# One load line for matrices and weights, and smaller weight steps, in the first stage of a fused diffusion block

## Chip, cores and metric

The kernel runs on one core of one Trainium2 chip. The metric is the device time of one launch in microseconds (us), as the median of runs. TensorE, VectorE, ScalarE, GpSimd and SyncE are called PE, DVE, ACT, POOL and SP in the profile; a DMA is issued by one of them into its queue.

## What is computed

One layer of a transformer block over 512 latent tokens of width 2048 (and 256 context tokens), in float32. Cut to what the first stage needs:

```
shift, scale, gate = split(silu(c) @ w_ada + b_ada, 3)       # modulation, per channel
h  = rmsnorm(x, norm_g) * (1 + scale) + shift                # 512 x 2048
p  = h @ w_in                                                # q, k, v, z_a, u_b, z_b, gates
y_b = (fourier_mix(u_b) * silu(z_b)) @ w_pb                  # branch B
...                                                          # attention branch A, merge, w_o, residual, final norm
```

The first stage makes `h` (transposed: 16 row blocks of 128 channels, each by 512 tokens) and from it u_b and z_b, eight strips of 128 columns of `w_in`. The Fourier part follows, then the large products.

## The kernel before

Each float32 operand of a product is split into a high and a low part (`split_from`: ACT writes the high part, L162, DVE the low part, L163), and one product is three matmuls (`mm3`, L296 to L298).

**A row block.** For block `kb`, `modulation(kb)` loads a matrix of 2 MB as two halves (`wada_load`, L416; tile `wa`, four buffers, so that two blocks fit) and multiplies it by the two condition vectors (L484, 16 matmuls for each half, 32 in all). ACT copies the sum (L491), PE turns it with two transposes (L494), and DVE reduces it and makes shift and gain (L500, L537, L538). `make_h` then scales the row on DVE (L472), writes the high part on ACT (L473) and the low part on DVE (L474). From then on the block can be multiplied.

**The weights.** The eight strips come in pieces of up to 512 KB (`start_pieces`, tile `wr`, four raw buffers), with the rows grouped as in

```
GROUPS = [(0, 1), (1, 1), (2, 2), (4, 4), (8, 4), (12, 4)]      # (first row block, how many)
```

A piece holds one group's rows for as many strips as fit. Strips 0 to 3 (u_b) keep a sum each in PSUM over all rows (`pb`). Strips 4 to 7 (z_b) are summed in PSUM over one group only (`pc`, two banks) and then added to `part`: by ACT's copy for the first row (L511), by DVE's addition later (L513). `start_work` is a generator that yields after each strip; the loop over `kb` draws from it up to what is owed, which counts whole groups only, and at most 32 matmuls a round.

**The loads.** Pieces are issued on SP. They are taken from the list `todo` by `load_more`, as far as raw buffers are free. The matrices of blocks 0 and 1 are issued on SP too, those of blocks 2 to 15 on POOL. `split_piece` splits pieces when `get` asks for them, `look` pieces ahead; in rounds 2 and 3 one further piece is split behind the row's own instructions (`tc.issue_after`).

**The order.** A scheduler places each engine's instructions from the order in which the program names them, their dependences and costs of its own; each engine then runs its list in order. `tc.issue_after(i)` keeps the next instructions behind `i`.

Of the kernel before, what the change touches and what calls it, by code (L numbers as in the profile page):

```python
# [18 lines left out]
P = 128  # L19
# [3 lines left out]
KK = D // P  # L23
# [13 lines left out]
START = [O_UB + P * i for i in range(4)] + [O_ZB + P * i for i in range(4)]  # L37
NS = len(START)

GROUPS = [(0, 1), (1, 1), (2, 2), (4, 4), (8, 4), (12, 4)]  # L40
RAW = 4

HL, MORE_HL = 3, 2
# [21 lines left out]
def context_piece(g, name, pc):  # L65

    n = 28 * (g - NQZ) + 4 * ONE_GROUP.index(name) + pc
    if n % 2 == 0 and 0 <= n < 8:
        return "cn", n // 2
    if n % 6 == 0 and 18 <= n < 42:  # L70
        return "cr", n // 6 - 3
# [18 lines left out]
def start_pieces():  # L90


    off, r = 0, []
    for kb, nk in GROUPS:
        per = 8 // nk
        new = [(kb, nk, t, min(per, NS - t)) for t in range(0, NS, per)]
        if kb == 0:

            new = [(0, 1, 0, 2), (0, 1, 2, 6)]
        for p in new:  # L100
            cols = p[1] * p[3] * P
            r.append((off, cols) + p)
            off += cols * P
    return r


# [1 line left out]
def block_kernel(ctx, tc, xT, ctx_rows, ctx_toks, x, c_row, w_ss, w_gate, vecs, qkg, rope, dft_c, dft_s,  # L108
                 w_start, w_g, w_pab, w_o, final_g, out):
    nc = tc.nc  # L110
# [8 lines left out]
    wp = sb("wp")  # L119
# [18 lines left out]
    def uid(s):  # L138
        cnt[0] += 1
        return f"{s}{cnt[0]}"  # L140
# [8 lines left out]
    def hm_tile(shape, dt, name):  # L149
        return slot(hm, shape[1:], dt)  # L150
# [4 lines left out]
    def bank2():  # L155
        return ps.tile([P, 512], F32, tag="b2", bufs=2, name=uid("pd"))
# [4 lines left out]
    def split_from(src, hi, lo):  # L161
        nc.scalar.activation(hi, src, ACT.Copy)  # L162
        return nc.vector.tensor_tensor(lo, src, hi.bitcast(F32), op=ALU.subtract)  # L163


    todo, ahead = [], []
# [16 lines left out]
    def start_load():  # L183

        e = todo[0]
        if callable(e):
            if e():
                todo.pop(0)
                return True
            return False  # L190
        used = [p for a in ahead for p, _ in a.raws]
        free = [p for p in raw_pools for _ in range(p[1] - used.count(p))]
        if len(e.parts) > len(free) or e.stage == 0 and (not chain or left[e.pc]):
            return False
        todo.pop(0)
        for p, src in zip(free, e.parts):
            raw = p[0].tile([P, 1024], F32, tag=p[2], bufs=p[3], name=uid("wr"))[:, : e.cols]
            nc.sync.dma_start(raw if len(src.shape) == 2 else raw.rearrange("p (i j c) -> p i j c", i=4, j=2), src)
            e.raws.append((p, raw))
        if e.stage == 0:  # L200
            nc.sync.dma_start(chain[e.pc], e.first)
            left[e.pc] = 1
        ahead.append(e)
        return True

    def load_more():
        while todo and len(ahead) < 8 and start_load():
            pass

    class Halves:  # L210

# [10 lines left out]
    def hl_tiles():  # L222
        hl_pools.append(hl_pools.pop(0))
        pool = hl_pools[-1]
        if isinstance(pool, tuple):
            return [slot_tile(p, (1024,), F32R) for p in pool]
        if isinstance(pool, int):
            return int_tiles(pool)
        return [pool.tile([P, 1024], F32R, tag=t, bufs=hl_pools.count(pool), name=uid("w" + t)) for t in ("hi", "lo")]
# [3 lines left out]
    look = [1]  # L233

    def split_piece(e):
        if e.out is not None or e.kind == "raw":
            return
        raws = [r for _, r in e.raws]
        src = raws.pop(0) if e.stage is None else chain[e.pc]
        for r in raws:  # L240
            nc.vector.tensor_tensor(src, src, r, op=ALU.add)
        if e.off:
            nc.vector.tensor_tensor(src, chain[e.pc], src, op=ALU.subtract)
        hi, lo = e.dst() if e.dst else hl_tiles()
        if isinstance(hi, Halves):
            for k in range(2):
                split_from(src[:, 512 * k : 512 * k + 512].rearrange("p (a c) -> p a c", a=2), hi.parts[k], lo.parts[k])
        else:
            hi, lo = hi[:, : e.cols], lo[:, : e.cols]
            last_split[0] = split_from(src, hi, lo)  # L250
        if e.nxt is not None:
            nc.gpsimd.dma_start(chain[e.pc], e.nxt, accum_op=ALU.add)  # L252
        if e.stage == 3:
            left[e.pc] = 0
        r = lambda t: t if isinstance(t, Halves) else t.rearrange("p (n m) -> p n m", n=e.n)
        e.out = (r(hi), r(lo))
# [111 lines left out]
    for g in range(LAST + 1):  # L368
        for name in ONE_GROUP:
# [6 lines left out]
            for pc in range(4):  # L376
                p = context_piece(g, name, pc)
                if p:
                    src, cols = (ctx_toks[p[1]], 1024) if p[0] == "cn" else (ctx_rows[p[1]], 4 * C)
# [14 lines left out]
    for name in OUT_GROUP:  # L394
        stream_product(name, 8, w_o[1], BY_DVE_OUT)
        if name in DONE:
            half, c = DONE[name]
            stream(("x", half, 2 + c), flat(x[half, 2 + c]), 1024, 1, "raw")
    for name in ONE_GROUP:
        stream_product(name, 9, w_o[0], BY_DVE_OUT)  # L400
        half, c = {"P2": (0, 0), "P7": (1, 1), "Q3": (1, 0)}.get(name, (0, 0))
# [11 lines left out]

    def wada_load(kb, h):
        w = pap.tile([P, 8, 256], F32, tag="wada", bufs=4, name=uid("wa"))
        (nc.gpsimd if kb > 1 else nc.sync).dma_start(w, w_ss[kb, :, 8 * h : 8 * h + 8, :])  # L416
        return w

    for a, n in XCH:
# [39 lines left out]
    def spread(pick, r):  # L459
# [2 lines left out]
            nc.tensor.matmul(acc[:, t * P : t * P + P], pick[:, t, :], r, start=True, stop=True)  # L462
        return acc

    wada = {(0, h): wada_load(0, h) for h in range(2)}
    while todo and len(ahead) < 3:
        start_load()
    wada.update({(1, h): wada_load(1, h) for h in range(2)})

    def make_h(hi, lo, src, rr, kb, j):  # L470
        tmp = src
# [6 lines left out]
    def matvec(acc, pieces):  # L478

        kk = 0  # L480
        for w in pieces:
            for k in range(w.shape[1]):
                j = kk % 4
                nc.tensor.matmul(acc[32 * j : 32 * j + 32, :256], c2[:, kk, :], w[:, k, :],  # L484
                                 start=kk < 4, stop=kk >= KK - 4)
                kk += 1

    def columns(acc, kb):

        o = pap.tile([P, 256], F32, tag="ada_o", bufs=2, name=uid("ado"))  # L490
        nc.scalar.copy(o, acc[:, :256])  # L491
        sp = acc[:, 256:]
        for i in range(2):
            turned = nc.tensor.transpose(sp[:, P * i : P * i + P], o[:, P * i : P * i + P], ident)  # L494
        if kb == 0:
            with tc.issue_after(turned.ins):
                rx0.append(spread(*norms))
            warm(3, o)
        r = pap.tile([P, 2, 2], F32, tag="ada_r", bufs=2, name=uid("adr"))
        nc.vector.tensor_reduce(r, sp.rearrange("p (h g r) -> p h r g", h=2, g=4)[:, :, 0:2, :], axis=AX.X, op=ALU.add)  # L500
        return r
# [30 lines left out]

    def modulation(kb):
        acc = bank2()
        matvec(acc, [wada.pop((kb, h), None) or wada_load(kb, h) for h in range(2)])
        sp = columns(acc, kb)
        nc.vector.tensor_scalar(shift[:, kb, :], sp[:, 0, :], bada[:, kb : kb + 1], None, op0=ALU.add)  # L537
        nc.vector.tensor_scalar(gain[:, kb, :], sp[:, 1, :], bsc1[:, kb : kb + 1], ng[:, kb : kb + 1],  # L538
                                op0=ALU.add, op1=ALU.mult)
# [18 lines left out]
    for kb in range(KK):  # L558
        if kb:
            modulation(kb)  # L560
        if kb % 2 == 0:
            pairs.append([hm_tile([P, 2, T], F32R, name=uid(n)) for n in ("hh", "hl")])
        hhi[kb], hlo[kb] = (t[:, kb % 2, :] for t in pairs[-1])
        ins = make_h(hhi[kb], hlo[kb], xt[:, kb, :], rx if kb else rx0[0], kb, 0)
        if kb >= 8:
            form_row(kb - 8)
        if kb == 0:
            nc.scalar.copy(rx, rx0[0])
            split_piece(ahead[0])
            with tc.issue_after(ins[1].ins):  # L570
                for e in ahead[1:3]:
                    split_piece(e)

        full = max([k + n for k, n in GROUPS if k + n <= kb] or [0])
        owed = 24 * full
        lim = min(owed, done + 32)
        while done < lim:
            done += next(work)
        if kb in (2, 3):
            with tc.issue_after(ins[1].ins), tc.issue_after(ins[2].ins):  # L580
                split_piece(next(e for e in ahead if e.out is None))
            look[0] = 2 * kb - 2
    while next(work):
        pass
    pa.close()
    rp = ctx.enter_context(tc.tile_pool(name="rp", bufs=1, reuse_waits="tile"))
    chain += [rp.tile([P, 1024], F32, name=f"R{pc}") for pc in range(4)]
# [18 lines left out]
    raw = get(("dftc", 0))  # L606
# [270 lines left out]
    class Context:  # L877
# [8 lines left out]
        def begin(self, name):  # L886
            self.f = get(("cf", name))
            if name == "Q5":
                nc.sync.dma_start(self.K.rearrange("p (h d) -> p h d", h=4), qkg[:, 2:3, :].broadcast_to([P, 4, HD]))
# [296 lines left out]
    for i in range(NSTEP + 3):  # L1186
        h, t = divmod(i, 4)
# [381 lines left out]
```

## Time and profile before

| | us |
|---|---|
| three runs | 1332.83, 1335.85, 1336.69 |
| median | 1335.85 |
| the profiled execution | 1333.12 |
| its span, first to last instruction | 1331.3 |

The span is what the views of the profile divide; the profiled execution's time holds 1.8 us more around it. In a timeline row stand start, duration, engine, line, operation, output and inputs, shape and count; in brackets the idle time of the engine just before, and what ended it. A matmul's duration runs past the start of the next, since they are pipelined; its cost is the distance between starts.

### The profile page before, as it was taken

To read this page: it belongs to the slowest core of one execution; us is meant where nothing else is said; L and a number is where in the kernel's file an instruction comes from. 1 tells how busy PE (TensorE), PEld (TensorE's weight loads), DVE (VectorE), ACT (ScalarE), POOL (GpSimd) and SP (SyncE) were. 2 spreads that over 40 slices of the span, in tenths; PEclk is the share of its full clock that TensorE was granted. 3 is DMA by queue.
4 is the path that set the end of the run, shared out by engine and by line. 5 is a ranking of instruction groups with operands and counts; after the bars stand their busy time and mean duration, and the time that the engine had idled before them with its cause. 6 is when DMAs were issued, how large, how long until landed. Compare 5 with 4: busy or idle time off the path is not lost. (4 is left out here: it accounts for less than half of the span.)

```text
span 1331.3 us, 17479 instructions
## 1 busy us (share of the span) xinstructions
PE 1298.5 (98%) x6594; PEld 1061.9 (80%) x6594; DVE 977.9 (73%) x1286; ACT 653.2 (49%) x1017; POOL 137.1 (10%) x186
## 2 busy tenths in 40 slices
PE   6999999999999999999999999999999999999996
PEld 3566888888888887888887888788888888887885
DVE  4655989887778867646477666677776789777677
ACT  5322655555555544544264455666665133364444
POOL 1110011210302011011021110000000100111210
PEclk9999999999999999999999999999999999999999
DMA  9996677887897999777669886122113899678983
GB/s 380 402 387 243 227 190 197 228 230 223 195 317 189 304 268 267 255 166 182 190 181 308 217 240 227 31 71 80 43 53 112 328 329 333 181 172 224 224 216 142
DMA packets 96085, 291.28 MB, mean 219 GB/s; under 512 B 8960, under 2 KB 32000, under 8 KB 91648
## 3 DMA queue, kind: packets, MB, share of 16 engines
q1 hardware_dynamic: 51600, 172.95, 37.1%
q0 software_dynamic: 21936, 94.39, 29.0%
q10 hardware_dynamic: 22464, 22.81, 5.1%
q8 instruction: 52, 0.85, 0.3%
q14 instruction: 33, 0.27, 0.1%
HBM read 263.37 MB, written 26.75 MB: 218 GB/s over the span
## 5 line engine op out<-in xcount | busy, mean ns | idle before, releaser
L162 ACT ACTIVATE whi<-wr 128x1024 fp32r<-128x1024 f32 (+1 forms) x130 | 136.6, 1052 | 189.8 <-PE y L298 90.0
L296 PE MATMUL y<-whi,s 128*128 128x512 f32 x548 | 216.4, 395 | 1.1 <-ACT s L768 1.1
L297 PE MATMUL y<-wlo,s 128*128 128x512 f32 x548 | 214.0, 390 | 0.7 <-DVE wlo L163 0.7
L296 PE MATMUL x<-whi,s 128*128 128x512 f32 x548 | 214.1, 391 | 0.2 <-ACT s L765 0.2
L297 PE MATMUL x<-wlo,s 128*128 128x512 f32 x548 | 213.5, 390 | 0.1
L298 PE MATMUL y<-whi,s 128*128 128x512 f32 x548 | 213.4, 390 | 0.0
L298 PE MATMUL x<-whi,s 128*128 128x512 f32 x548 | 213.3, 389 | 0.0
L163 DVE TENSOR_TENSOR wlo<-wr,whi 128x1024 fp32r<-128x1024 f32 (+1 forms) x130 | 157.0, 1211 | 57.6 <-ACT whi L162 57.4
L162 ACT ACTIVATE whi<-R 128x1024 fp32r<-128x1024 f32 x115 | 121.6, 1059 | 128.3 <-PE y L298 55.5
L163 DVE TENSOR_TENSOR wlo<-R,whi 128x1024 fp32r<-128x1024 f32 x115 | 139.7, 1220 | 48.9 <-ACT whi L162 48.9
L296 PEld LDWEIGHTS y<-whi,s 128*128 128x128 f32 x548 | 102.9, 188 | 24.9 <-DVE s L1166 2.3
L296 PEld LDWEIGHTS x<-whi,s 128*128 128x128 f32 x548 | 102.9, 188 | 21.8 <-ACT s L765 0.5
L297 PEld LDWEIGHTS x<-wlo,s 128*128 128x128 f32 x548 | 102.9, 188 | 21.7 <-DVE wlo L163 0.6
L298 PEld LDWEIGHTS y<-whi,s 128*128 128x128 f32 x548 | 102.9, 188 | 21.6
L298 PEld LDWEIGHTS x<-whi,s 128*128 128x128 f32 x548 | 102.9, 188 | 21.4
L297 PEld LDWEIGHTS y<-wlo,s 128*128 128x128 f32 x548 | 103.0, 188 | 20.4 <-DVE wlo L163 1.1
L296 PE MATMUL x<-s,s 128*128 128x512 f32 (+1 forms) x274 | 104.5, 381 | 4.2 <-ACT s L1126 3.1
L297 PE MATMUL x<-s,s 128*128 128x512 f32 (+1 forms) x284 | 106.5, 375 | 0.0
L298 PE MATMUL x<-s,s 128*128 128x512 f32 (+1 forms) x284 | 106.1, 374 | 0.0
L252 POOL DMA_DIRECT2D R<-in_w_g x64 | 55.2, 863 | 423.6 <-DVE wlo L163 263.2
L162 ACT ACTIVATE s<-wr 128x512 fp32r<-128x512 f32 (+2 forms) x92 | 60.4, 675 | 57.4 <-PE y L298 17.2
L163 DVE TENSOR_TENSOR s<-wr,s 128x512 fp32r<-128x512 f32 (+2 forms) x92 | 65.8, 743 | 23.3 <-ACT s L162 21.8
(275 smaller groups left out, 2249.0 us busy)
## 6 DMA issues: line engine op xcount, KB each, us to landing
wr<-in_w_g SPq DMA_DIRECT2D x128, 512.0 KB, 4.9
R<-in_w_g POOLq DMA_DIRECT2D x64, 512.0 KB, 6.7
wa<-in_w_ss POOLq DMA_DIRECT2D x28, 1024.0 KB, 9.1
R<-in_w_g SPq DMA_DIRECT2D x32, 512.0 KB, 5.1
wr<-in_w_pab SPq DMA_DIRECT2D x32, 512.0 KB, 5.1
wr<-in_w_gate SPq DMA_DIRECT2D x32, 512.0 KB, 5.5
wr<-in_w_o SPq DMA_DIRECT2D x24, 512.0 KB, 6.9
R<-in_w_o POOLq DMA_DIRECT2D x24, 512.0 KB, 7.4
```

The lines of the kernel that those rows point to most:

```text
L162: nc.scalar.activation(hi, src, ACT.Copy)
L163: return nc.vector.tensor_tensor(lo, src, hi.bitcast(F32), op=ALU.subtract)
L252: nc.gpsimd.dma_start(chain[e.pc], e.nxt, accum_op=ALU.add)
L296: nc.tensor.matmul(o, ah, bh, start=start, stop=False, skip_group_check=cont)
L297: nc.tensor.matmul(o, ah, bl, start=False, stop=False, skip_group_check=cont)
L298: nc.tensor.matmul(o, al, bh, start=False, stop=stop, skip_group_check=cont)
```

## The change

The steps are written out. Rows 0 to 3 come one by one, rows 4 to 11 in twos, and of the last four rows strips 0 to 3 in twos and strips 4 to 7 in one group. The round owes each step as soon as its rows are made. All loads of the stage, matrices too, are issued on SP, each kept behind the one before it: after each matrix follow as many pieces as `BEHIND` says. A matrix is asked for when the one two blocks earlier has been multiplied. From round 2 on, each round splits one piece behind its row's own instructions, and `look` stays at 1 until the stage ends.

```diff
-GROUPS = [(0, 1), (1, 1), (2, 2), (4, 4), (8, 4), (12, 4)]
+STEPS = ([(0, 1, 0, 2), (0, 1, 2, 6)] + [(k, 1, 0, 8) for k in range(1, 4)]
+         + [(k, 2, t, 4) for k in range(4, 12, 2) for t in (0, 4)] + [(12, 2, 0, 4), (14, 2, 0, 4)]
+         + [(12, 4, t, 2) for t in (4, 6)])
+BEHIND = {**{k: 1 for k in range(2, 14)}, 14: 2, 15: 2}
...
-            nc.sync.dma_start(raw if len(src.shape) == 2 else raw.rearrange("p (i j c) -> p i j c", i=4, j=2), src)
+            dst = raw if len(src.shape) == 2 else raw.rearrange("p (i j c) -> p i j c", i=4, j=2)
+            begin = lambda: nc.sync.dma_start(dst, src)
+            if may[0] < 1000:
+                in_line(begin)
+            else:
+                begin()
...
+    may, last_load = [0], [None]
+
+    def in_line(dma):
+        if last_load[0] is None:
+            last_load[0] = dma()
+        else:
+            with tc.issue_after(last_load[0].ins):
+                last_load[0] = dma()
+
     def load_more():
-        while todo and len(ahead) < 8 and start_load():
-            pass
+        while todo and len(ahead) < 8 and may[0]:
+            if not start_load():
+                break
+            may[0] -= 1
...
-        (nc.gpsimd if kb > 1 else nc.sync).dma_start(w, w_ss[kb, :, 8 * h : 8 * h + 8, :])
+        in_line(lambda: nc.sync.dma_start(w, w_ss[kb, :, 8 * h : 8 * h + 8, :]))
...
-    wada = {(0, h): wada_load(0, h) for h in range(2)}
-    while todo and len(ahead) < 3:
-        start_load()
-    wada.update({(1, h): wada_load(1, h) for h in range(2)})
+    wada = {}
+
+    def load_block(kb):
+        if kb < KK:
+            wada.update({(kb, h): wada_load(kb, h) for h in range(2)})
+            may[0] += BEHIND.get(kb, 0)
+        load_more()
+
+    load_block(0)
+    may[0] = 3
+    load_more()
+    load_block(1)
...
-        matvec(acc, [wada.pop((kb, h), None) or wada_load(kb, h) for h in range(2)])
+        matvec(acc, [wada.pop((kb, h)) for h in range(2)])
+        load_block(kb + 2)
...
-        full = max([k + n for k, n in GROUPS if k + n <= kb] or [0])
-        owed = 24 * full
+        owed = 0
+        for k, nk, t, nt in STEPS:
+            if k + nk > kb:
+                break
+            owed += 3 * nk * nt
         lim = min(owed, done + 32)
         while done < lim:
             done += next(work)
-        if kb in (2, 3):
-            with tc.issue_after(ins[1].ins), tc.issue_after(ins[2].ins):
-                split_piece(next(e for e in ahead if e.out is None))
-            look[0] = 2 * kb - 2
+        if kb >= 2:
+            e = next((e for e in ahead if e.out is None), None)
+            if e and e.kind == "wp":
+                with tc.issue_after(ins[1].ins), tc.issue_after(ins[2].ins):
+                    split_piece(e)
     while next(work):
         pass
+    may[0] = 1000000
+    look[0] = 4
```

13 lines of the change are left out of this document (4 added, 9 removed).

## Prediction

> **What bounds the kernel now.** The page comes first: TensorE is busy for nearly the whole span, so only idle time and extra work of TensorE can move the total. The table by stage comes second, with cuts where the first stage starts its products, where its early part ends, where the Fourier part begins and where that ends.
>
> ```profile
> PE 1298.5 (98%) x6594; PEld 1061.9 (80%) x6594; DVE 977.9 (73%) x1286; ACT 653.2 (49%) x1017; POOL 137.1 (10%) x186
> core 0: us, PE busy (x) PEld busy (x) DVE busy (x) ACT busy (x) POOL busy (x), PEclk, DMA share, GB/s
> 0.00:24.10 24.10, 14.43 (x64) 6.93 (x64) 11.70 (x27) 15.08 (x27) 3.16 (x13) 1.00 0.93 367
> 24.10:50.30 26.20, 23.75 (x176) 14.24 (x176) 13.84 (x26) 7.93 (x14) 3.77 (x7) 1.00 1.02 418
> 50.30:154.20 103.90, 103.88 (x720) 72.29 (x719) 69.58 (x129) 37.62 (x56) 10.21 (x19) 1.00 0.83 322
> 154.20:172.00 17.80, 17.55 (x146) 17.35 (x145) 13.52 (x20) 7.55 (x13) 0.55 (x1) 1.00 0.50 147
> ```
>
> Up to 24.10 us nothing changes: the first loads stand in the same order in both kernels. From 24.10 to 50.30 TensorE idles 26.20 - 23.75 = 2.45 us. From 50.30 to 154.20 it idles 0.02 us, though the DMA engines are busy 83% of that time, and in the Fourier part 0.25 us. All that better loading can win therefore lies in those 2.45 us. Third, the waits of TensorE between 24 and 155 us, the rows of the first and of the largest, and the matrices' time from issue to landing:
>
> ```profile
> PE pd L484 <- DMA wa<-in_w_ss: 2.4, 3, 1.4
> 29.91 1.07 PE L484 MATMUL pd<-wa,c 128*32 128x256 f32 x16 [0.37 <-DMA wa<-in_w_ss]
> 46.15 0.59 PE L484 MATMUL pd<-wa,c 128*32 128x256 f32 x2 [1.39 <-DMA wa<-in_w_ss]
> DMA to landing us min/median/max: 5.1/9.4/16.6
> wa<-in_w_ss POOLq DMA_DIRECT2D x28, 1024.0 KB, 9.1
> ```
>
> Three waits, all for modulation matrices that share the DMA engines with weight pieces on the other queue. This is what the fixed line can remove.
>
> **What the change does to each row.** Each row block runs one chain: two halves of the modulation matvec (L484), ScalarE copies the sum (L491), TensorE turns it (L494), VectorE makes shift, gain and the scaled row (L500 to L472), ScalarE writes the high half (L473), and only then can TensorE multiply the row. TensorE runs in written order, so what stands between the links decides whether the chain is hidden. Its length is read from the last row, in the timeline:
>
> ```profile
> 129.54 0.39 PE L298 MATMUL pc<-s,wlo 128*128 128x512 f32 x1
> 129.86 1.93 PE L484 MATMUL pd<-wa,c 128*32 128x256 f32 x32
> 131.73 0.50 PE L296 MATMUL pb<-s,whi 128*128 128x512 f32 x1
> 132.06 0.40 PE L297 MATMUL pb<-s,whi 128*128 128x512 f32 x1
> 132.53 0.38 PE L494 MATMUL pd<-ident,ado 128*128 128x128 f32 x2
> 132.67 0.47 PE L296 MATMUL pb<-s,whi 128*128 128x512 f32 x1
> 132.98 0.39 PE L297 MATMUL pb<-s,whi 128*128 128x512 f32 x1
> 133.02 0.17 DVE L500 TENSOR_REDUCE adr<-pd 128x4 f32<-128x16 f32 x1 [0.91 <-PE pd L494]
> 133.21 0.40 PE L298 MATMUL pb<-s,wlo 128*128 128x512 f32 x1
> 133.68 0.75 DVE L472 SCALAR_TENSOR_TENSOR xt<-xt,gain,rx 128x512 f32<-128x512 f32 x1
> 134.47 0.72 ACT L473 ACTIVATE s<-xt,shift 128x512 fp32r<-128x512 f32 x1 [2.18 <-DVE xt L472]
> 18.57 2.07 PE L484 MATMUL pd<-wa,c 128*32 128x256 f32 x32
> 21.23 0.41 PE L494 MATMUL pd<-ident,ado 128*128 128x128 f32 x2 [0.58 <-ACT ado L491]
> ```
>
> From the turn at 132.53 to the end of the high half at 134.47 + 0.72 = 135.19, and 0.05 us for the signal (an estimate), is 2.71 us. A turn takes 0.14 us of TensorE (132.53 to 132.67), the next matmul 0.31 and each further one 0.23 (132.67, 132.98, 133.21). So with n matmuls behind the turn TensorE stands still for 2.71 - 0.14 - 0.31 - 0.23(n - 1), and with none for 2.57. From matvec to turn, row 0 shows the bare latency: end at 18.57 + 2.07 = 20.64, turn at 21.23, which is 0.59. As 131.73 lies 0.06 before the end of its matvec (129.86 + 1.93), a turn straight behind a matvec idles 0.65; three matmuls hide that.
>
> In the kernel before, the groups of four rows left dozens of matmuls to stand there. The built order of the changed kernel on TensorE has this many:
>
> ```
> row          before its turn   between turn and the row's first matmul
> 1            3                 4 and half a matvec
> 2, 3, 4      3                 11 to 14 and half a matvec
> 5            3                 3
> 6, 8, 10, 12 3                 20 or more and half a matvec
> 7            3                 7
> 9, 11        3                 8
> 13           3                 9
> 14           0                 0
> 15           0                 0
> ```
>
> A pair's products have only the first row's matmuls to offer while the second row's chain runs, and part of them is spent ahead of the turn. By the formula row 5 stands 1.80, row 7 0.88, rows 9 and 11 0.65 each, row 13 0.42; row 1 has 0.14 + 0.31 + 3 x 0.23 + 1.09 (half a matvec, below) = 2.23 of cover and stands 0.48. Together 4.9 us. Rows 14 and 15 have nothing in hand, since the last four rows' strips 4 to 7 come only later: 0.65 + 2.57 = 3.22 each, 6.4 us. **Chains: 11.3 us.** This is the term that decides. An end below it is 6.4 (only the bare rows), one above needs further gaps.
>
> **Cut matvecs.** Between the halves the built order now always has matmuls. One half alone costs:
>
> ```profile
> 69.76 0.40 PE L296 MATMUL pb<-s,whi 128*128 128x512 f32 x1
> 70.08 1.07 PE L484 MATMUL pd<-wa,c 128*32 128x256 f32 x16
> 71.08 0.50 PE L297 MATMUL pb<-s,whi 128*128 128x512 f32 x1
> 71.42 0.39 PE L298 MATMUL pb<-s,wlo 128*128 128x512 f32 x1
> ```
>
> From 69.76 to 71.42 less two matmuls at 0.23 is 1.20 us; 1.09 of it (70.08 less the 0.09 delay, to 71.08) stands before the next matmul. A whole one takes 129.54 to 132.06 = 2.52, less 0.46, which is 2.06. A cut costs 2 x 1.20 - 2.06 = 0.34. The order before has 9 cuts (six rows, three single pieces), the new one 16: 7 x 0.34 = **2.4 us**, nearly sure, as TensorE's own time.
>
> **More additions on VectorE.** Strips 4 to 7 are added up per step: nine steps in place of six, 4 x 3 = 12 more additions.
>
> ```profile
> L513 DVE TENSOR_TENSOR part<-pc,part 128x512 f32<-128x512 f32 x19 | 12.9, 685 | 6.5 <-PE pc L298 6.3
> ```
>
> 12 x 0.685 = 8.2 us, beside TensorE's work where VectorE is busy 69.58 of 103.90 us. It reaches TensorE through the two banks: the third strip waits until the first is added. In rows 2 and 3, TensorE is there 0.14 + 0.31 + 7 x 0.23 = 2.06 after the turn; VectorE has the scaled row first (133.68 + 0.75 = 1.90 after it) and then the addition, 2.58. That is 0.5 each, as for row 1's products; in the pairs from 8 on, where a strip has six matmuls, 0.3 three times. Between 0 (if the addition slips ahead) and 2.4; I take **1.8**.
>
> **The tail.** Strips 6 and 7 of the last rows now come behind two Fourier channels, and need a bank that VectorE frees by an addition. In the kernel before:
>
> ```profile
> 147.44 0.68 DVE L513 TENSOR_TENSOR part<-pc,part 128x512 f32<-128x512 f32 x1
> 154.20 0.28 PE L296 MATMUL pb<-fch,uh 128*128 128x256 f32 x1
> 154.31 0.28 PE L297 MATMUL pb<-fch,uh 128*128 128x256 f32 x1
> L163 DVE TENSOR_TENSOR wlo<-wr,whi 128x1024 fp32r<-128x1024 f32 (+1 forms) x16 | 19.1, 1205 | 5.1 <-ACT whi L162 5.1
> ```
>
> That addition ends 147.44 + 0.68 - 135.19 = 12.9 us behind the last high half, and the new order puts one more split of 1.2 us ahead of it. TensorE is there after 36 matmuls at 0.23 and 24 at 0.11 to 0.12 (154.20, 154.31), 11.2 us. So it waits 2.9, or 0 if VectorE closes its idle places on the way; I take **2.0**, nearer the upper end.
>
> **What costs nothing.** The 28 issues of matrix halves that stand on POOL move to SP. There a matrix now waits until TensorE has read the one two rows before it, and the piece and all later loads stand behind that wait. Who would feel it is the matvec two rows on. Over 15 us of TensorE work lie between (two rows of 24 x 0.23 + 2.06), while 2 MB and a 0.5 MB piece take 2.62 MB / 418 GB/s = 6.3 us. At the start, the bytes up to the end of row 1's matrix are 9.5 MB; at 367 GB/s it lands at 26 us, ahead of its use, which today waits until 29.91. So loading does not bind, and the splits, one per row behind the row, are ready a row early.
>
> **Sum.** The profiled execution took 1333.12 us, its span 1331.3. Less 2.5 for the waits, plus 11.3, 2.4, 1.8 and 2.0: 1333.1 + 15.0 = **1348.1 us**. The profiled execution lies near the low end of the three runs (median 1335.85), so a median 2 to 3 us above the sum would be no surprise.
>
> **A rule that speaks against it.** Bare gaps could also slow the clock. TensorE's start shows it:
>
> ```profile
> 8.81 0.50 PEld L451 LDWEIGHTS pd<-s,ones 128*128 128x128 f32 x2 [8.81 <-DVE s L450]
> ...
> 13.24 0.34 PEld L451 LDWEIGHTS pd<-s,ones 128*128 128x128 f32 x1 [0.52 <-DVE s L447]
> 14.10 0.28 PEld L451 LDWEIGHTS pd<-s,ones 128*128 128x128 f32 x1 [0.52 <-issue]
> 14.62 0.19 PEld L451 LDWEIGHTS pd<-s,ones 128*128 128x128 f32 x1 [0.24 <-DVE s L450]
> 513.67 0.50 PE L297 MATMUL y<-s,s 128*128 128x512 f32 x1 [2.17 <-DVE s L163]
> 514.01 0.40 PE L298 MATMUL y<-s,s 128*128 128x512 f32 x1
> 514.25 0.39 PE L296 MATMUL y<-s,s 128*128 128x512 f32 x1
> ```
>
> After the opening idle a weight load took 0.34 us until 13.24 and 0.19 from 14.62, though the clock column says 1.00; behind an idle of 2.17 us matmuls follow every 0.24 at once. A gap of 2.57 with one more just before it lies past what the trace bears out. The Trainium skill, "TensorE: Matmul & The Clock Gate", section "Why this matters for your kernels", says that idle gaps above about 3 us put TensorE back to half clock.
>
> **Rivals.** (1) *Faster*: the matrices' waits go and the chains stay hidden, as they are now. Then 1333.1 - 2.5 = 1330.6, or less gain with some cuts. For it: no wait behind 50 us today. Against: the built order leaves rows 14 and 15 bare. It decides if turn to first matmul takes under 0.6 us rather than 2.71. Chance 0.06. (2) *Half*: only the two bare rows stand, banks and tail are covered: 1333.1 - 2.5 + 6.4 + 2.4 = 1339.4; 0.14. (3) *Clock*: both bare rows lose half of some 5 us (the slow loads stand from 8.81 to 14.10): 1348.1 + 5.3 = 1353.4; 0.14. (4) *The line binds*: a piece held on SP holds all matrices; if each lands 1 us late, as the 16.6 us landing above would make it against 15 us of cover, 13 rows give 13 us: 1361; 0.04. (5) That the line is not kept is excluded: SP's built order shows it.
>
> **Chances.** The forecast has 0.62, with 1344 to 1353 for its unsure terms. The range from 1338 to 1358 takes in (2), (3) and the median's offset and leaves out (1) and (4). About 0.3%, 4 us, can be told from no change: slower needs over 1339.9, which the forecast, (3), (4) and somewhat under half of (2) give, 0.86; within it 0.08; faster 0.06.
>
> **What would show it.** Right: TensorE idle before the first matmul of rows 5, 7, 9, 11, 13 (0.4 to 1.8) and of 14 and 15 (about 2.6), released by ScalarE L499 in the new line numbers; no wait for the matrices; a wait for an addition ahead of strip 6; all 15 matvecs in two parts; the Fourier part ending 15 us later than 172. Wrong: TensorE as full as before behind 50 us, or waits for DMA in the matvecs.

## The result, and the profile after

The changed kernel took 1353.51 us (median of 4 runs, 1352.83 to 1355.08), the kernel before beside it 1334.34 us. The ratio is 1.0149, with an interval of 1.0131 to 1.0167: slower by 1.5%. The profiled execution took 1353.17 us.

The page of the changed kernel, for the span and TensorE's line, and its table by stage:

```profile
span 1351.4 us, 17460 instructions
...
PE 1307.7 (97%) x6594; PEld 1061.9 (79%) x6594; DVE 984.2 (73%) x1298; ACT 652.3 (48%) x1017; POOL 121.0 (9%) x158
```

```profile
24.10:50.30 26.20, 25.27 (x172) 15.40 (x172) 13.84 (x27) 7.61 (x13) 0.00 (x0) 1.00 1.01 403
50.30:100.00 49.70, 46.93 (x336) 29.21 (x335) 28.99 (x58) 10.62 (x17) 0.00 (x0) 1.00 0.86 300
100.00:140.00 40.00, 38.62 (x264) 24.18 (x263) 23.20 (x45) 9.85 (x14) 0.00 (x0) 1.00 0.88 305
140.00:172.00 32.00, 24.69 (x133) 17.24 (x132) 18.99 (x36) 16.59 (x25) 0.00 (x0) 0.84 0.47 186
172.00:190.30 18.30, 18.30 (x139) 17.60 (x138) 17.70 (x26) 7.32 (x12) 0.71 (x1) 1.00 0.39 128
```

TensorE's busy share fell by one point only, but the span grew by 20.1 us. The table says where: up to 50.30 us TensorE idles less than before (0.93 us against 2.45), and behind it, where it idled for 0.27 us up to 172, 2.77, 1.38 and 7.31 us appear. From 140 to 172 the granted clock is 0.84 as well, so that "busy" there is partly slow work. The Fourier part ends at the first matmul of the large products, at 171.97 us before and at 190.34 after:

```profile
171.97 0.40 PE L296 MATMUL x<-whi,s 128*128 128x512 f32 x1
```

```profile
190.34 0.40 PE L313 MATMUL x<-whi,s 128*128 128x512 f32 x1
```

That is 18.4 us. The rest, some 1.8 us by the rounded spans, comes behind it: from that matmul to the end of the span are 1331.3 - 171.97 = 1159.3 us before and 1351.4 - 190.34 = 1161.1 us after.

TensorE's waits from 24 to 200 us, now without a matrix among them:

```profile
PE pb L313 <- ACT s L499: 9.0, 9, 2.4
PE pc L313 <- DVE part L539: 2.3, 4, 1.4
PE pd L520 <- ACT ado L517: 1.1, 2, 0.5
```

The matrices themselves came sooner after their issue, in a median of 5.4 us against the 9.1 that those on POOL took before:

```profile
wa<-in_w_ss SPq DMA_DIRECT2D x32, 1024.0 KB, 5.4
```

And the rows of its timeline in which the gaps stand (row 5's turn and first product, row 7's, then rows 14 and 15, then strip 6):

```profile
64.07 0.38 PE L520 MATMUL pd<-ident,ado 128*128 128x128 f32 x2
...
66.78 0.97 PE L313 MATMUL pb<-s,whi 128*128 128x512 f32 x3 [1.63 <-ACT s L499]
...
84.11 0.73 PE L313 MATMUL pb<-s,whi 128*128 128x512 f32 x2 [0.71 <-ACT s L499]
...
141.97 0.44 PE L520 MATMUL pd<-ident,ado 128*128 128x128 f32 x2 [0.55 <-ACT ado L517]
144.84 2.07 PE L313 MATMUL pb<-s,whi 128*128 128x512 f32 x4 [2.44 <-ACT s L499]
146.85 1.94 PE L510 MATMUL pd<-wa,c 128*32 128x256 f32 x16
...
153.18 0.44 PE L520 MATMUL pd<-ident,ado 128*128 128x128 f32 x2 [0.55 <-ACT ado L517]
155.95 1.19 PE L313 MATMUL pb<-s,whi 128*128 128x512 f32 x4 [2.33 <-ACT s L499]
...
170.37 0.50 PE L313 MATMUL pc<-s,whi 128*128 128x512 f32 x1 [1.44 <-DVE part L539]
```

From 64.07 to 66.78 are 2.71 us, the chain from turn to first product. With three matmuls in it, 1.63 us of it is shown idle. Rows 14 and 15 have none and idle 0.55 ahead of the turn as well as 2.44 and 2.33 behind it. Row 14's products come with a second sign: half a matvec, 1.07 us wherever TensorE is at full speed, takes 1.94 at 146.85.

### The profile page after: what moved, and what is told of

It reads as the page before. It is cut to its first block, busy times and chain, and to the rows that moved or that the text cites. A ratio compares the mean times of both kernels' runs of the same rounds, so it can differ in the third digit from the quotient of the medians.

```text
span 1351.4 us, 17460 instructions
## 1 busy us (share of the span) xinstructions
PE 1307.7 (97%) x6594; PEld 1061.9 (79%) x6594; DVE 984.2 (73%) x1298; ACT 652.3 (48%) x1017; POOL 121.0 (9%) x158
## 4 chain that ended last, share of the span: by engine, by line
PE 76%; DVE 10%; DMA 7%; ACT 4%; issue 3%; ACTq 0%; POOL 0%; DVEq 0%; SPq 0%
PE y L313 11%; PE y L314 11%; PE y L315 11%; PE x L313 10%; PE x L314 10%; PE x L315 10%; DVE wlo L162 3%; PE tp L1176 2%; PE pd L510 2%; DMA wr<-in_w_g 2%; PE pb L313 2%; PE pb L314 1%; DVE s L162 1%; PE pb L315 1%; DMA cf_d<-qr 1%
```

## The experiments

In the table, "stage" runs from the first product of row 0 to the first matmul of the large products, "rest" from there to the end of the span, both in the profiled execution; "low" is the time between 24 and 200 us at a granted clock of 0.50, summed from narrow windows of each trace. Ratios are against the kernel before on the same chip, with their interval.

| kernel | median us | ratio | stage us | rest us | low us |
|---|---|---|---|---|---|
| before | 1333 to 1336 | 1 | 147.85 | 1159.3 | 0 |
| after | 1353.51 | 1.0149 (1.0131 to 1.0167) | 166.53 | 1161.1 | 10.2 |
| e1 steps only | 1337.30 | 1.0014 (1.0001 to 1.0027) | 146.98 | 1162.3 | 0 |
| e2 line only | 1351.38 | 1.0110 (1.0086 to 1.0133) | 163.66 | 1163.0 | 6.8 |
| e3 last rows held | 1346.21 | 1.0071 (1.0047 to 1.0095) | 157.35 | 1163.1 | 0 |
| e4 whole matrices | 1349.49 | 1.0105 (1.0078 to 1.0131) | 155.80 | 1164.4 | 6.8 |
| e5 matrices on POOL | 1335.69 | 1.0031 (1.0020 to 1.0043) | 148.38 | 1161.4 | 3.4 |
| e6 before, matrices on SP | 1350.87 | 1.0132 (1.0116 to 1.0148) | 162.81 | 1161.6 | 6.8 |
| e7 before, whole matrices | 1335.63 | 1.0024 (1.0009 to 1.0038) | 146.63 | 1158.9 | 0 |
| e8 fed gaps | 1349.09 | 1.0123 (1.0110 to 1.0136) | 162.66 | 1161.4 | 0 |
| e9 paced, matrices on POOL | 1332.19 | 0.9993 (0.9982 to 1.0004) | 146.96 | 1160.3 | 0 |
| e10 line, whole, held | 1340.90 | 1.0064 (1.0046 to 1.0081) | 155.32 | 1158.8 | 10.0 |
| e11 paced, whole | 1332.71 | 0.9993 (0.9982 to 1.0005) | 148.16 | 1160.4 | 0 |
| e12 line, held | 1338.74 | 1.0036 (1.0023 to 1.0049) | 153.17 | 1160.9 | 3.4 |

Before, the stage begins at 24.12 us, in e4, e7 and e10 at 25.94, 26.18 and 27.16, in the others at 23.4 to 23.95; the span holds that, the stage does not. The ratio is estimated from all runs of both kernels, and so is not everywhere the quotient of two medians. The column "low" is one execution of each kernel, and the last section shows why another can differ. The rest of e2 and of e4 holds a low stretch as well, at 531 and 528 us.

**e1: the small steps alone.** The kernel before with the list of steps of the change and what it owes by them; loads, queues and splits as before.

```diff
-GROUPS = [(0, 1), (1, 1), (2, 2), (4, 4), (8, 4), (12, 4)]
+STEPS = ([(0, 1, 0, 2), (0, 1, 2, 6)] + [(k, 1, 0, 8) for k in range(1, 4)]
...
-        full = max([k + n for k, n in GROUPS if k + n <= kb] or [0])
-        owed = 24 * full
+        owed = 0
+        for k, nk, t, nt in STEPS:
+            if k + nk > kb:
+                break
+            owed += 3 * nk * nt
```

> The new steps (single rows to row 3, then twos) with the old loads: matrices on POOL, pieces on SP without a line, old splitting. Theory A (the bare chains come from the order that the planner makes for the single line, not from the small steps): its built order has at least ten matmuls, or some with matvec halves, behind every turn but row 5's, and only 4 cut matvecs; so against before: waits for matrices stay (0), five cuts fewer -1.7, row 5 +1.2, banks +1.8, tail +2: about +3.3 us, 1337, no clock drop. Theory B (small steps alone leave the chains bare): as the changed kernel, +19 us, 1353.

The waits of TensorE from 24 to 195 us:

```profile
PE pc L293 <- DVE part L510: 2.0, 1, 2.0
PE y L294 <- DVE wlo L160: 1.8, 1, 1.8
PE pd L481 <- DMA wa<-in_w_ss: 1.3, 3, 0.7
```

No chain stands bare: no wait for ScalarE's high half (L499 in the changed kernel) is in the list. The steps alone shorten the stage by 0.9 us and lose 3.0 us behind it. So the small steps alone do not cost the 20 us.

**e2: the fixed line alone.** The changed kernel with the old groups in place of the small steps.

```diff
-STEPS = ([(0, 1, 0, 2), (0, 1, 2, 6)] + [(k, 1, 0, 8) for k in range(1, 4)] + ...
+STEPS = ([(0, 1, 0, 2), (0, 1, 2, 6), (1, 1, 0, 8), (2, 2, 0, 4), (2, 2, 4, 4)]
+         + [(k, 4, t, 2) for k in (4, 8, 12) for t in range(0, 8, 2)])
```

> The one load line, its pace and the splits behind own rows, with the old steps (1, 1, 2, 4, 4, 4 rows). Theory A: the built order leaves 2, 2 and 3 matmuls behind the turns of rows 3, 5 and 6, 4 behind row 11's and all 16 matvecs cut: chains 9.0 us, seven cuts 2.4, waits for matrices -2.5, so about +9 us against before, 1343; rows 13 to 15 are covered, so no clock drop. Theory B (the line itself only helps): -2.5 us, 1331.

It lost most of what the whole change loses, and more than expected: the stage is 15.8 us longer. Two of its gaps:

```profile
48.99 1.19 PE L312 MATMUL pb<-s,whi 128*128 128x512 f32 x3 [1.86 <-ACT s L498]
...
68.01 0.73 PE L312 MATMUL pb<-s,whi 128*128 128x512 f32 x2 [1.86 <-ACT s L498]
```

With groups of four, which left no such wait behind row 0 in the kernel before, the chains of rows 3, 5, 6 and 11 now stand bare (6.0 us). Here the cover is gone though the work is there: the planner, that is, the scheduler, places it elsewhere. Weight pieces that ScalarE came late to split cost another 2.7 us of waits, and two low stretches (49.58 to 52.98 and 107.60 to 111.02 us) came on top.

**e3: work kept for the last two rows.** The changed kernel, with the products of rows 12 and 13 behind the turn of row 14, and those of 14 and 15 behind the turn of row 15.

```diff
+        turn_of[kb] = turned.ins
...
-        while done < lim:
-            done += next(work)
+        with tc.issue_after(turn_of[kb if kb == 14 else 0]):
+            while done < lim:
+                done += next(work)
...
-    while next(work):
-        pass
+    with tc.issue_after(turn_of[KK - 1]):
+        while next(work):
+            pass
```

> The changed kernel, with the matmuls of rows 12 and 13 (strips 0 to 3) kept behind row 14's turn and those of rows 14 and 15 and the rest behind row 15's turn; nothing else. If rows 14 and 15 cost what the changed kernel's trace shows: their bare chains go (2.4 + 2.3), two cuts fewer (0.7) and both stretches at half clock (4.2): -9.6 us against the changed kernel, 1344. If the clock falls for another reason than these gaps: -5.4 us, 1348.

The Fourier part ended at 180.73, 9.6 us earlier than after the change. The stage began 0.4 earlier, so the stage itself is 9.2 us shorter, against 9.6 expected, and in the profiled execution the low clock is gone. But the rest took 2.0 us more, so that the time fell by some 7 us only.

**e4: no cuts.** The changed kernel with each matrix as one transfer of 2 MB in two buffers, so that no matvec can be cut.

```diff
-        w = pap.tile([P, 8, 256], F32, tag="wada", bufs=4, name=uid("wa"))
-        in_line(lambda: nc.sync.dma_start(w, w_ss[kb, :, 8 * h : 8 * h + 8, :]))
+        w = pap.tile([P, KK, 256], F32, tag="wada", bufs=2, name=uid("wa"))
+        in_line(lambda: nc.sync.dma_start(w, w_ss[kb]))
...
```

> The changed kernel, with each modulation matrix loaded as one 2 MB transfer into two buffers in place of two halves into four. All matvecs are then whole in the built order: 16 cuts fewer at 0.34 us is -5.4; chains: row 1 covered (-0.4), row 5 has 5 matmuls (-0.5), row 15 has 3 (-0.7): about -7 us against the changed kernel, 1346.5. Rival: the cuts cost nothing in the end, or the larger transfers land too late and matvecs wait: no gain, 1352 to 1356, with waits for the matrices in the trace.

The stage is 10.7 us shorter, though it begins 2.1 us later. Sixteen cuts at 0.34 are 5.4 us, and of 10.2 us at the low clock 3.4 are left within the stage (the other low stretch comes at 193 us, behind it). Row 14 stays bare (2.44 us), and row 15 has three matmuls now. This fits the price of a cut but does not measure it alone, since order and clock moved too.

**e5: the matrices back on POOL.** The changed kernel with one line of it undone.

```diff
-        in_line(lambda: nc.sync.dma_start(w, w_ss[kb, :, 8 * h : 8 * h + 8, :]))
+        (nc.gpsimd if kb > 1 else nc.sync).dma_start(w, w_ss[kb, :, 8 * h : 8 * h + 8, :])
```

> The changed kernel with one thing undone: the sixteen matrices from block 2 on are loaded through GpSimd's queue again, as before; small steps, splits behind own rows and the pacing of the other loads stay. Theory A (matrices in SP's line make the planner hold the matvecs back to the last moment, and so leave the chains between turn and first product bare): the rows are covered again, no clock drop, some waits for the matrices return; 1337 us (1334 to 1340), some 16 us below the changed kernel. Theory B (the small steps, the splits or the paced loads leave too little work): within 3 us of 1353.5.

```profile
PE pc L313 <- DVE part L539: 1.9, 1, 1.9
PE pd L510 <- DMA wa<-in_w_ss: 1.3, 1, 1.3
PE y L314 <- DVE wlo L162: 0.4, 1, 0.4
```

Theory A. One line, which moves fourteen matrices (28 transfers), takes back 18.2 of the stage's 18.7 us; the chains are covered, and a wait for matrices of 1.3 us returns. The waits that are left belong to the tail: an addition ahead of strip 6 (1.9 us, and a low stretch right behind it) and VectorE behind the Fourier part.

**e6: the matrices on SP, and nothing else.** The kernel before with the opposite edit.

```diff
-        (nc.gpsimd if kb > 1 else nc.sync).dma_start(w, w_ss[kb, :, 8 * h : 8 * h + 8, :])
+        nc.sync.dma_start(w, w_ss[kb, :, 8 * h : 8 * h + 8, :])
```

> The kernel before with one thing done: the sixteen matrices go through SP's queue instead of GpSimd's, with no fixed line, the old groups and the old splits. Theory A (that queue alone is the cause): waits for matrices go (-2.5 us), the uncovered parts of the chains come to 7.8 us (rows 1, 3, 5 to 7, 14 and 15), six more cut matvecs 2.0, additions waited for and lag behind the Fourier part 3.5, a clock drop after row 15's bare chain up to 2: 11 to 13 us over the kernel before, 1347 us. Theory B (the queue only brings the matrices sooner): 2.5 us below the kernel before, 1333 us.

```profile
PE pb L296 <- ACT s L473: 7.3, 7, 2.3
PE pb L296 <- ACT whi L162: 2.4, 1, 2.4
PE pc L296 <- DVE part L513: 1.9, 2, 1.4
```

Theory A again, at the far end of it: the stage is 15.0 us longer. The chains' 7.3 us are near the expected 7.8, though rows 8 and 12 stand bare (0.86 and 0.63) in place of rows 5 to 7; a late split (2.4) and a low stretch of 6.8 us were not expected. TensorE waits for no transfer in this list; what has changed for it is the built order. It shows, between a row's turn and its first product, this many matmuls (h for half a matvec):

```
row                          7      9      11     13     14     15   cut matvecs
before                       6+h    43+5h  8+h    60+4h  27+2h  10   9
after                        7      8      8      9      0      0    16
e1, e5 (matrices on POOL)    12+2h  12+2h  12+2h  12+2h  21+2h  10   4
e6 (before, matrices on SP)  6+h    13+h   6+h    13+h   8      0    15
```

**e7: whole matrices on the old queues.** The kernel before, with e4's edit.

```diff
-        w = pap.tile([P, 8, 256], F32, tag="wada", bufs=4, name=uid("wa"))
-        (nc.gpsimd if kb > 1 else nc.sync).dma_start(w, w_ss[kb, :, 8 * h : 8 * h + 8, :])
+        w = pap.tile([P, KK, 256], F32, tag="wada", bufs=2, name=uid("wa"))
+        (nc.gpsimd if kb > 1 else nc.sync).dma_start(w, w_ss[kb])
...
```

> The kernel before with each matrix loaded as one transfer of 2 MB instead of two of 1 MB, on the same queues, in two buffers instead of four. By the price of a cut (0.34 us for each matvec in two parts) seven fewer cuts bring 2.4 us: 1333 us. The rival: with two whole buffers instead of four halves a matrix can only start when a whole one is free and its first half is not usable alone, so waits for matrices grow by 1 to 5 us: 1336 to 1341.

```profile
26.18 1.21 PE L296 MATMUL pb<-s,whi 128*128 128x512 f32 x4 [0.30 <-ACT s L473]
...
63.90 1.93 PE L484 MATMUL pd<-wa,c 128*32 128x256 f32 x32 [1.09 <-DMA wa<-in_w_ss]
```

The stage is 1.2 us shorter: seven fewer cuts (2.4) less 1.3 us more waits for matrices (3.7 against 2.4, four of them, as the one at 63.90). That fits the price of a cut: 1.2 + 1.3 = 2.5 for seven. The gain is lost ahead of the stage, which begins 2.06 us later since the first matvec has to wait for 2 MB.

**e8: the gaps fed.** The changed kernel with four matmuls of no use in each of the two bare chains, two waiting for `shift` and two for `gain`; nothing reads them. The trace shows each of them as two records.

```diff
+        if kb >= 14:
+            for part in (shift, gain):
+                for _ in range(2):
+                    nc.tensor.matmul(acc[:16, :256], part[:, kb - 7 : kb + 1, :].rearrange("p k j -> p (k j)"),
+                                     c2[:, 0:8, :].rearrange("p k j -> p (k j)"), start=True, stop=True)
```

> The changed kernel with four small matrix products of no use (128x256 moving columns, 16 stationary) put into each of the two bare chains of rows 14 and 15, two of them waiting for shift, two for gain, so that TensorE is not idle for more than about 1 us at a stretch; their results are never read and the chains stay as long. The theory that the lower granted clock of 144 to 152 and 156 to 162 us comes from these gaps: the clock stays at 1.0 there and the time falls by about 4 us, to 1349.3. The rival, that the clock falls there for another reason (the load of work in all, or the four-part alternation that follows): the clock falls as before, time 1353.5 or up to 1 us more.

```profile
141.66 0.44 PE L520 MATMUL pd<-ident,ado 128*128 128x128 f32 x2 [0.55 <-ACT ado L517]
142.69 1.04 PE L570 MATMUL pd<-c,shift 128*16 128x256 f32 x4 [0.60 <-DVE shift L564]
143.57 1.03 PE L570 MATMUL pd<-c,gain 128*16 128x256 f32 x4
144.55 0.96 PE L313 MATMUL pb<-s,whi 128*128 128x512 f32 x3
...
150.44 0.44 PE L520 MATMUL pd<-ident,ado 128*128 128x128 f32 x2 [0.55 <-ACT ado L517]
```

```profile
100.00:150.00 50.00, 47.37 (x334) 28.14 (x332) 25.60 (x51) 10.94 (x16) 0.00 (x0) 1.00 0.71 251
150.00:200.00 50.00, 45.98 (x268) 39.46 (x269) 42.79 (x63) 31.26 (x44) 2.11 (x3) 1.00 0.60 208
```

The clock stays at 1.00, though the chains are as long as they were (turn at 141.66, first product at 144.55) and TensorE does more work. The Fourier part ends at 186.21, 4.13 us earlier, of which 0.31 were there before row 14's turn. The work behind the gaps shows the price of the clock: from row 14's first product to row 15's turn it takes 5.89 us here and 8.34 in the changed kernel, from row 15's first product to the first matmul of the Fourier part 8.32 and 9.95, together 4.1. The gaps' length cost 6.6 us; that TensorE was idle in them cost another 4.1. This is not one execution's chance: the mean granted clock is 0.997 or 0.998 in all four executions of e8, and 0.994 or 0.995 in all four of the changed kernel.

**e9: the line without the matrices, old groups.** The changed kernel with e2's and e5's edits together.

> The old groups with the change's other parts but two: the pieces are paced (one behind each matvec) and split behind own rows, but the matrices stay on GpSimd's queue. Its order on TensorE is that of the kernel before, rows all covered, strips ahead of the Fourier channels. Theory A (queue of the matrices is what costs; pacing the pieces gives the matrices' transfers more of the DMA engines): some of the 2.4 us of matrix waits goes, nothing else moves: 0 to 2.4 us below the kernel before, 1332.5. The rival (pacing or the later splits cost something by themselves): pieces or splits come too late for their rows, 2 us or more above the kernel before.

Waits for matrices fell from 2.4 us to 1.9, the stage by 0.9 us, and the rest rose by 1.0. The time cannot be told from the kernel before: neither a gain nor the cost that the rival named shows.

**e10: all in one line, whole matrices, products held.** e2's and e4's edits, and each round's products held behind the turn of the row before, so that every chain keeps some.

```diff
...
-        while done < lim:
-            done += next(work)
+        with tc.issue_after(turn_of[kb if kb == 14 else max(kb - 1, 0)]):
+            while done < lim:
+                done += next(work)
```

> All loads in SP's one line as in the change, but the old groups, each matrix as one transfer of 2 MB, and the products of a group held behind the turn of the row before, so that the planner must keep work for the chains; strips lie ahead of the Fourier channels again. If theory A is the whole story, a line that is kept from baring the rows beats the kernel before: waits for matrices -2.5, nine fewer cut matvecs -3.1, no bare chain but row 3's and part of row 7's (+0.7), no lag behind the Fourier part: some 4 to 5 us below the kernel before, 1329. The rival: the held products make gaps of their own ahead of the matvecs, or the 2 MB matrices come late in two buffers (the whole-matrix kernel on the old queue had 3.7 us of such waits): at or above the kernel before, 1333 to 1338.

```profile
72.72 3.64 PE L509 MATMUL pd<-wa,c 128*32 128x256 f32 x32 [4.46 <-DMA wa<-in_w_ss]
```

A miss: one whole matrix came 4.46 us late, and the clock fell in that gap (a matvec of 32 takes 1.93 us at full speed). Six copies ahead of a turn stand bare as well (3.9 us in all). The rival came true, and by more than its 1338 us: with two whole buffers one late transfer binds, and the held products left gaps of their own, though ahead of the turns.

**e11: an attempt at a faster version.** e9 with matrices of 2 MB for blocks 2 to 15; those of blocks 0 and 1 come in two transfers.

```diff
+        w = pap.tile([P, KK, 256], F32, tag="wada", bufs=2, name=uid("wa"))
+        if kb > 1:
+            nc.gpsimd.dma_start(w, w_ss[kb])
+        else:
+            for i in (0, 8):
+                nc.sync.dma_start(w[:, i : i + 8, :], w_ss[kb, :, i : i + 8, :])
```

> An attempt at a version that beats both: the old groups, pieces paced and split behind own rows, the matrices of blocks 2 to 15 on GpSimd's queue and each as one transfer of 2 MB; blocks 0 and 1 come in two transfers, so that the first matvec does not start later (with whole first matrices the part began 2.06 us later). Seven fewer cut matvecs (-2.4) against 1 to 2 us more waits for whole matrices, pacing -1: 1 to 2.5 us below the kernel before, 1331. The rival: the waits for whole matrices eat the gain, within 1 us of the kernel before.

```profile
PE pd L513 <- DMA wa<-in_w_ss: 5.2, 6, 1.8
```

The stage begins at 23.62 again, but the waits for whole matrices, 5.2 us, eat what seven cuts gave. No version beats the kernel before by more than can be measured.

**e12: all in one line, halves, products held.** e10 with the matrices in halves and four buffers.

> All loads in SP's one line, the old groups, matrices in halves as in the change, and the products of a group held behind the turn of the row before; strips ahead of the Fourier channels. The waits for matrices go (-2.4), no chain from turn to first product is bare, but the copy ahead of the turn is, in seven rows (0.55 us each, +3.9), and 0.4 us of the chains of rows 3, 7 and 15 (+1.2); no clock drop, no lag behind the Fourier part: 2 to 3 us over the kernel before, 1335.5, and 11 to 18 us below the line without the hold. The rival (the line itself is bad, whatever the order: the transfers come late or the queue costs): as much over the kernel before as the line with the old groups was, 13 to 16 us, 1348.

```profile
65.85 0.44 PE L519 MATMUL pd<-ident,ado 128*128 128x128 f32 x2 [1.67 <-ACT ado L516]
...
70.14 0.65 PE L519 MATMUL pd<-ident,ado 128*128 128x128 f32 x2 [1.99 <-ACT ado L516]
```

There is no wait for a matrix at all, nor one for a split, and the stage is 10.5 us shorter than in e2, the same line without the hold. The line's transfers therefore come in time, and most of what e2 lost, it lost by order. What stays against the kernel before (5.3 us of stage) is mainly the bare copies ahead of the turn, in seven rows as expected but 6.4 us in all: 0.55 in five of them, 1.67 and 1.99 in two, where a matvec is followed by its turn with nothing between. There ScalarE splits a weight piece before it comes to the copy:

```profile
64.50 1.04 ACT L160 ACTIVATE whi<-wr 128x1024 fp32r<-128x1024 f32 x1
65.45 0.35 ACT L516 COPY ado<-pd 128x256 f32<-128x256 f32 x1
```

A low stretch of 3.4 us stands behind those two rows.

## Why the prediction was right, and where it was not

The forecast, 1348.1 us, was 5.1 below the profiled execution; the side and the deciding term were right. The time lies within the wide range, 1338 to 1358, but just above the 1344 to 1353 that the forecast gave itself, and on the 1353.4 of rival (3). By its own steps, measured as the distance between starts where rows are named:

| term | predicted us | measured us | from |
|---|---|---|---|
| waits for matrices | -2.5 | -2.8 | none left; the three before, with their distance between starts |
| bare chains | +11.3 | +11.4 | starts of turn and first product in each row |
| cut matvecs | +2.4 | 2.5 for seven | e7 |
| additions ahead of banks | +1.8 | +2.1 | rows at 39.76, 49.28 and 58.07 us (1.4), 92.64, 110.08 and 127.51 (0.25 each) |
| the tail | +2.0 | +1.6 | row at 170.37 |
| lower clock | rival (3): +5.3 | +4.1 | e8 |
| start of the stage | 0 | -0.3 | 23.81 against 24.12 us |
| a wait in the Fourier part | 0 | -0.4 | before alone, for DVE al L163 |
| behind the Fourier part | 0 | +1.8 | the rest of the span |

The measured terms add up to 20.0, the span's growth is 20.1. The five terms of the forecast make 14.8 of it against 15.0 predicted; the miss is the clock and the stretch behind the Fourier part. That the total fell on rival (3)'s 1353.4 is luck: its clock term was 1.2 too large, and 1.8 us came from a stretch for which no term stood.

**The order.** Each wait that was forecast stands in the trace at its place: rows 5, 7, 9, 11 and 13 by 0.24 to 1.63 us, released by ScalarE L499, rows 14 and 15 by over 2.3, and the addition ahead of strip 6. The chain's 2.71 us, read from one row of the trace before, is in each of the rows that the new order left bare (2.71 to 2.87).

**Why the rows are bare: wrong.** The prediction put it down to the small steps ("a pair's products have only the first row's matmuls to offer", "rows 14 and 15 have nothing in hand"). e1 and e5 have the same steps and cover every one of these rows. Nor did the groups of four leave dozens of matmuls everywhere: row 7 had six and half a matvec, row 15 ten, which is just enough. The step that failed stands under "What costs nothing": the matrices' move to SP was weighed as a transfer only, and as a transfer it does cost nothing (5.4 us to landing, and no wait for a matrix in the changed kernel, in e6 and in e12). But the order of TensorE's list hangs on it. e5 and e6 show that from both sides: this one line takes 18.2 us off the changed kernel's stage and puts 15.0 on that of the kernel before. That the scheduler reckons the matrices to land later on SP, and so puts each matvec behind the products that should have covered its chain, is inferred from the built orders; no run shows the costs that it reckons with. The sum held all the same, since its fills were counted in the built order and not derived from that reason.

**The clock: a rival that came true beside the forecast.** Rival (3) had the mechanism and 5.3 us for it, and was given 0.14. Against it stood a gap of 2.17 us without harm in the trace before. That row was no evidence: the gap lay across two stretches of the clock's grid, in which TensorE was still busy 0.67 and 0.69 of the time (the last section has the grid). The term was 4.1, not 5.3: the low stretches were 6.8 and 3.4 us long, and part of the first fell on idle time.

**Behind the Fourier part: a term that was missing.** The account ended with the tail. Splits by VectorE now come late for the first large products:

```profile
PE y L314 <- DVE wlo L162: 1.0, 1, 1.0
PE x L314 <- DVE s L162: 0.9, 1, 0.9
```

The first stands 12 us behind the Fourier part, the second 55. Before, TensorE's first wait behind it comes after 342 us. A wait for a low part 11 to 13 us behind the Fourier part (0.4 to 2.3 us) is in all eight kernels whose last strips come behind the first Fourier channels (after, e1 to e6, e8) and in none of the six that keep the strips ahead (before, e7, e9 to e12); the second, of 0.9, is in seven of the eight. The rest in the table parts the same way, 1161.1 to 1164.4 us against 1158.8 to 1160.9, but with only 0.2 us between. That the tail's order does this is argued from this split; no run moved the tail alone.

**The rivals that fell.** One reading was off: the first of the three waits before, at 29.91, was for block 1, whose matrix already stood on SP. It went with the others. Rival (1) needed covered chains; (2) needed the banks and rows 5 to 13 covered; (4) needed late matrices, and there was no such wait. The remark that a median 2 to 3 us above the sum would be no surprise was not needed: profiled execution and median lie 0.3 us apart.

## What to carry to other kernels

Where a planner writes the order, moving a load to another queue is a change of order. Count, in the built list, what stands between the links of each chain, and undo the queue alone before blaming the tiling. A change to the loads cannot win more than the waits for loads that the trace shows, here 2.4 us of 1331, while every chain that it lays bare costs what nothing covers of it. Where a gap in TensorE cannot be filled with useful work, a few small products in it can keep the clock up, as they did in e8.

## What the hardware showed unexpectedly

The granted clock has two values here, 1.00 and 0.50, and changes only at points 3.41 us apart. In the changed kernel it falls at 143.66, rises at 150.49, falls at 157.32 and rises at 160.73; in e2 it falls at 49.58 and 107.60, seventeen times 3.41 us apart. Every low stretch that ends between 24 and 200 us, in any of these runs, lasts 3.41 us or twice that. Cut along this grid, the table of windows shows what decides (length, TensorE's busy time, and far right granted clock, DMA share and rate); the changed kernel, then e4:

```profile
140.25:143.66 3.41, 1.60 (x19) 0.62 (x18) 1.10 (x5) 0.37 (x1) 0.00 (x0) 1.00 0.29 115
143.66:147.07 3.41, 2.23 (x8) 1.36 (x12) 1.61 (x3) 0.72 (x1) 0.00 (x0) 0.50 0.02 5
147.07:150.49 3.42, 3.42 (x20) 1.89 (x13) 0.00 (x0) 0.00 (x0) 0.00 (x0) 0.50 0.00 0
150.49:153.90 3.41, 2.58 (x23) 1.19 (x22) 0.17 (x1) 0.37 (x1) 0.00 (x0) 1.00 0.00 0
153.90:157.32 3.42, 1.37 (x6) 1.15 (x7) 2.88 (x8) 2.14 (x3) 0.00 (x0) 1.00 0.00 0
157.32:160.73 3.41, 3.41 (x10) 2.63 (x9) 3.27 (x6) 2.61 (x5) 0.00 (x0) 0.50 0.74 263
```

```profile
138.66:142.07 3.41, 1.60 (x7) 1.33 (x8) 2.23 (x5) 0.72 (x1) 0.00 (x0) 1.00 0.05 18
...
145.48:148.90 3.42, 1.60 (x6) 0.88 (x7) 2.35 (x7) 2.05 (x3) 0.00 (x0) 1.00 0.00 0
148.90:152.32 3.42, 3.42 (x9) 2.67 (x9) 2.25 (x3) 1.06 (x1) 0.00 (x0) 0.50 0.52 129
```

A stretch of 3.41 us in which TensorE was busy well under half is followed by a low one: 0.47 of 140.25 to 143.66, 0.40 of 153.90 to 157.32; in other runs 0.05 to 0.48 (e2, e4, e5, e6, e10, e12). Every stretch from 20 us to the last 12 us of a span that was busy under 0.45 was, and none above 0.48 (e12 at 63 had 0.51, after at 65 and e2 at 73 had 0.52). Between the two both happened: e4's rows show 1.60 us busy once without and once with a fall, and e9 has 0.45 at 509 us, e3 0.48 at 521 us without one. The clock stays low behind a low stretch that was busy 0.65 (143.66) or 0.77 (e6) and rises behind one of 0.84 or more.

So the length of a gap does not decide by itself, but also how it lies to the grid. The grid lies differently in each execution: counted in steps of 3.413 us (352 of them lie between the falls at 143.66 and 1345.15 us after the change), its first point is 0.30 us behind the start of the span in the profile after the change, 2.13 in e4's and 3.33 in e6's. The same gap can therefore cost one execution and spare another; over the twelve executions of e7 the mean granted clock goes from 0.994 to 0.998. An idle of 1.94 us within one stretch was enough in e5 (busy 0.43, fall at 151.42), while one of 2.0 us in e1 and those of 1.86 us at 68.01 in e2 and 2.17 us in the kernel before did no harm. A fall costs up to 1.7 us of TensorE's time for each 3.41 us.

The Trainium skill, "TensorE: Matmul & The Clock Gate", section "What's actually happening", has a free-running window of 3413 ns, with which these traces agree (3.41 us). Its section "Why this matters for your kernels" warns of idle gaps above about 3 us; here 1.94 us sufficed, and the measurement decides: TensorE's busy share of one window counts.
